# Issuing the sums of feed-forward values in one go, with later VectorE weight parts queued behind them

## The chip, the cores and the metric

The kernel runs on one core of a Trainium2 chip. A core has TensorE (matrix products; PE in the profile, with PEld for its weight loads), VectorE (DVE), ScalarE (ACT), GpSimd (POOL) and SyncE (SP, which here only issues transfers). The engines run side by side, each takes its own instructions in the order in which they stand in its stream, and they wait for each other through semaphores. The metric is the device time of one execution in microseconds (us); the median of three timed runs stands for a kernel. The profile is one further execution, recorded by the hardware, with its own time.

## The reference

One inference step of a hybrid encoder layer over 576 token rows (512 of a prompt, 64 of a sample):

```python
h   = x @ W_in                                   # queries, keys, values of two kinds of heads
mix = concat(ForgettingAttention(h_A), IndexedSparseAttention(h_B))
x   = LN1(alpha * x + mix @ W_o)
hid = relu(x @ W_up) ** 2                        # 1024 -> 4096
x   = LN2(alpha * x + hid @ W_down)              # 4096 -> 1024
x   = x + sigmoid(x @ W_g + b_g) * (p @ W_ple)
```

All is float32. The change concerns the feed-forward part, the lines of `hid` and `W_down`.

## The kernel before, in words

Tokens lie along the free axis, features along the 128 partitions. To keep float32 precision each factor of a product is split into a high part (a rounded copy, made by ScalarE) and a low part (the rest, a subtraction, mostly made by VectorE), and a product is three matmuls for each of its slices of 128 features: high by high, high weight by low value, low weight by high value (`gemm`, line 298; the matmuls have line 305).

**The stage of seven products.** The feed-forward width is cut into 8 groups of 512 (`NG`, line 386). Groups 0 and 1 are done plainly (`up`, line 1421). From group 2 on a block of W_up, two by two sub-blocks over two by two halves of the tokens and features, is done with seven products instead of eight, in the manner of Strassen and Winograd; so is W_down for groups 0 to 5 (`G_DOWN`, line 387, groups 6 and 7 go plainly through `down_last`). `seven` (line 1496) runs a list of pairs; each pair is seven products in the order 11, t0, t1, 21, t3, t2, 22, each of 12 matmuls, pinned to that order on TensorE. An even and an odd group of up pairs (two pairs each, m = 0 and 1) are followed by four down pairs that consume them (line 1684 on): up pairs of groups 2 and 3, four down pairs, up pairs of 4 and 5, four down pairs, up pairs of 6 and 7. There are two places, then, at which the second up pair of an odd group (3 or 5) hands over to down pair 0.

**The values between.** After each product a hook of the pair may run (`P.posts`). In an up pair (`up_pair`, line 1552) the hook of t2 adds two partial results on VectorE (L1573), squares the positive part (L1575 on VectorE for odd groups) and calls `operands` (line 1357). For an odd group that makes, from this value v and the values F of the even group, the operands of the down pairs: the second sum s2 = -F[0] - v (L1389) and its two parts (ScalarE L1368, VectorE L1366), the first sum s1 = F[1] - v (L1391) and its parts, the parts of v itself ("22"), and later "12" and "s4" (L1396). The down pair's products read them in this way (`ROWS`, line 1494): 11 reads "11", t0 "s3", t1 "s2", 21 "12", t3 "s1", t2 "22", 22 "s4". In the profile the tile hC holds s1 and s2, hA s3 and 11, hB 12 and 22, hD s4.

**What sets the order.** The hooks don't issue most of this at once. `later(delay, fn)` puts it on a list; `drive` (line 86) advances a clock by one for every six matmuls, and at each tick takes up to three entries that are due. So the steps are spread over the ticks after the product. The order in which the code issues instructions is the program's order; then the scheduler of the framework makes each engine's stream. It may take an instruction with a later number first where it reckons it ready sooner; `tc.high_priority()` raises what is issued inside it, and `tc.issue_after(ins)` makes what is issued inside it, on the engine of `ins`, stand behind `ins` in the stream, without waiting for its end.

**The weights.** `Weights` (line 117) streams the weights in. Each pair takes four units of weights from three loads (`add_seven`, line 171): r1 (two halves added by an accumulating transfer of GpSimd, L210), r2 and r3. A unit has a high part (ScalarE, L149) and a low part (VectorE, L155). Unit u is made from r2 as loaded, u+1 from r1; then VectorE adds r1 into the first half of r2 (`t1`, L181) and that half into the second (`t2`, L184); u+2 is made from these sums, u+3 (half as wide) from r3. Products 11 and 21 read u, t0 and t3 u+1, t1 and t2 u+2, and 22 reads u+3 (`PLACE`, line 105). These are pieces in a queue of the code; `WT.step()`, called after every six matmuls of a product, issues at most one, when its load has had time to land and buffers are free (`open`, line 220; a low part waits two ticks behind its high part, and the next piece may pass it). The raw buffers and the five buffers of parts (`whl`) go round in rings; a raw buffer that comes free lets SyncE issue the next load (L208).

The products wait for the parts they read by themselves: where a part is late, TensorE stands still at that matmul.

Of the kernel before, what the change touches and what calls it, by code (L numbers as in the profile page):

```python
# [11 lines left out]
OP = mybir.AluOpType  # L12
# [24 lines left out]
def tile_hybrid_step(ctx: ExitStack, tc: tile.TileContext, I, O):  # L37
    nc = tc.nc
    PE, ACT, DVE, POOL, SP = nc.tensor, nc.scalar, nc.vector, nc.gpsimd, nc.sync
# [4 lines left out]
    def f(ap):  # L44
        return ap.bitcast(F32)
# [16 lines left out]
    def later(delay, fn):  # L62
        number[0] += 1
        evq.append((clock[0] + delay, number[0], fn))
# [42 lines left out]
    class Unit:  # L107


        def __init__(self, t, c, o=0):  # L110
            self.t, self.c, self.o = t, c, o
# [5 lines left out]
    class Weights:  # L117
# [3 lines left out]
        def __init__(self):  # L121
            self.cs, self.loads, self.pieces = [], [], deque()
            self.raw_ring, self.raw_own, self.hl_ring, self.hl_own = {1024: [], 512: []}, {}, [], {}
            self.hv, self.done, self.oldest, self.loaded = {}, set(), 0, 0
            self.was, self.lag = deque([(0, 0)]), 1

        def ring(self, pool, n_raw, n_hl, name, n_small=0):
            self.raw_ring[1024] += [(pool, f"{name}raw{x}") for x in range(n_raw)]
            self.raw_ring[512] += [(pool, f"{name}rs{x}") for x in range(n_small)]
            self.hl_ring += [(pool, f"{name}hl{x}") for x in range(n_hl)]  # L130
# [10 lines left out]
        def split(self, u, src, cuts, eng):  # L141
            lo_at = [0]

            def high(c):
                def fn():
                    if c is cuts[0]:
                        self.slot(u)
                        lo_at[0] = clock[0] + 2
                    ACT.copy(self.hv[u][:, 0, c], src["tile"][:, c])  # L149
                return fn  # L150

            def low(c):
                def fn():
                    t = self.hv[u]
                    eng.tensor_tensor(t[:, 1, c], src["tile"][:, c], f(t[:, 0, c]), OP.subtract)  # L155
                    if c is cuts[-1]:
                        self.done.add(u)
                return fn
            for c in cuts:
                self.piece(u, None, high(c), src)  # L160
            for c in cuts:
                self.piece(u, lo_at if len(cuts) == 1 else None, low(c), src)
# [8 lines left out]
        def add_seven(self, ap):  # L171

            u = len(self.cs)
            self.cs += [128] * 4
            r1 = self.source(ap[:, 0:1024], acc=ap[:, 1024:2048])
            r2 = self.source(ap[:, 2048:3072])
            r3 = self.source(ap[:, 1024:1536], room=512)
            lo, hi, all2 = slice(0, 512), slice(512, 1024), slice(0, 1024)

            def t1():  # L180
                DVE.tensor_tensor(r2["tile"][:, lo], r2["tile"][:, lo], r1["tile"][:, lo], OP.add)  # L181

            def t2():
                DVE.tensor_tensor(r2["tile"][:, hi], r2["tile"][:, hi], r2["tile"][:, lo], OP.add)  # L184
            self.split(u, r2, [all2], DVE)
            self.split(u + 1, r1, [all2], DVE)
            self.piece(u + 1, None, t1, r1, r2)
            self.piece(u + 2, None, t2, r2)
            self.split(u + 2, r2, [all2], DVE)
            self.split(u + 3, r3, [lo], DVE)  # L190
            return u
# [87 lines left out]
    WT = Weights()  # L279
# [812 lines left out]
    for x, tag in ((0, "k32"), (1, "t2")):  # L1092
        t = sb.tile([128, NT], F32, name="praw", tag=tag)
# [235 lines left out]
    HX, late = {}, []  # L1329

    def sets(g):

        if g >= G_DOWN:
            hid[g] = base.tile([128, 2, 4, NT], F32R, name="hidE", tag="AL") if g % 2 == 0 else \
                fb.tile([128, 2, 4, NT], F32R, name="hidO", tag="hidO")
            return
        names = ("s3", "11") if g % 2 == 0 else ("12", "22")
        t = base.tile([128, 2, 2, 4, HW], F32R, name="hA", tag="AL") if g % 2 == 0 else \
            fb.tile([128, 2, 2, 4, HW], F32R, name="hB", tag="hidO")
        for i, n in enumerate(names):  # L1340
            HX[n] = [t[:, i, x] for x in range(2)]
        if g % 2 == 0:
            HX["f"] = fs.tile([128, 2, 4, HW], F32, name="hF")
# [10 lines left out]

    owed = {}

    def operands(g, m, t, v):

        b = slice(2 * m, 2 * m + 2)
        tt = DVE.tensor_tensor  # L1360

        def split(n, v, d=0):
            owed[n] = owed.get(n, 0) + 1

            def low():
                tt(HX[n][1][:, b], v, f(HX[n][0][:, b]), OP.subtract)  # L1366
                owed[n] -= 1
            later(d, lambda: ACT.copy(HX[n][0][:, b], v))  # L1368
            later(d, low)

        if g >= G_DOWN:
            oh, ol = [hid[g][:, x, b, (A, B)[t]] for x in range(2)]
            later(0, lambda: ACT.copy(oh, v))
            later(0, lambda: DVE.tensor_tensor(ol, v, f(oh), OP.subtract))
            return
        F = [HX["f"][:, x, b] for x in range(2)]
        if g % 2 == 0:
            if t == 0:
                split("11", v)
            if t == (g == 0):  # L1380
                later(3, lambda: tt(F[0], F[0], F[1], OP.subtract))
                split("s3", F[0], 3)
            return
        if t == 1:
            if m == 0:
                later(0, more_sets)
                if g > 1:
                    later(0, last_set)
            later(0, lambda: DVE.scalar_tensor_tensor(F[0], F[0], -1.0, v, op0=OP.mult, op1=OP.subtract))  # L1389
            split("s2", F[0])  # L1390
            later(1, lambda: tt(F[1], F[1], v, OP.subtract))  # L1391
            split("s1", F[1], 1)
            split("22", v, 3)
            return
        split("12", v)
        later(2, lambda: tt(v, v, F[0], OP.add))  # L1396
        if g > 1:
            split("s4", v, 2)
        else:
            late.append(lambda: split("s4", v, 2))  # L1400

    def up_half(g, c, m, sl):
        t = (A, B).index(sl)
        r = lnp[0].tile([128, 2, 320], F32, name="relu", bufs=2)[:, :, :HW]
        out = HX["f"][:, t, c:c + 2]
        later(0, lambda: ACT.activation(r, m[:, :, :HW], AF.Relu))
        later(0, lambda: ACT.activation(out, r, AF.Square))
        operands(g, c // 2, t, out)
# [132 lines left out]
    def owe(P, fn):  # L1541
        def do():
            fn()
            P.left -= 1
        P.left += 1
        later(0, do)

    def settle(P):
        while P.left:
            pop_now()  # L1550

    def up_pair(g, m):

        P = Pair(U["P", g // 2, g % 2 * 2 + m], SX)
        b = slice(2 * m, 2 * m + 2)
        tt = DVE.tensor_tensor
        if m == 0:
            P.start = lambda: sets(g)

        def target(t):  # L1560
            return HX["f"][:, t, b] if g < G_DOWN and g % 2 == 0 else P.r[:, t]

        def t0():
            P.r = fs.tile([128, 2, 2, HW], F32, name="r", bufs=2)
            owe(P, lambda: ACT.copy(P.r[:, 1, 0], P.z))

        def t3():
            settle(P)
            with tc.high_priority():
                tt(P.r[:, 1, 1], P.e, P.r[:, 1, 0], OP.subtract)  # L1570

        def t2():
            tt(P.r[:, 1, 0], P.o, P.r[:, 1, 0], OP.add)  # L1573
            if g % 2:
                later(0, lambda: DVE.scalar_tensor_tensor(target(1), P.r[:, 1], 0.0, P.r[:, 1], op0=OP.max, op1=OP.mult))  # L1575
            else:
                later(0, lambda: ACT.activation(P.r[:, 1], P.r[:, 1], AF.Relu))
                later(0, lambda: ACT.activation(target(1), P.r[:, 1], AF.Square))
            operands(g, m, 1, target(1))

        def s21():
            later(0, lambda: ACT.activation(P.r[:, 0, 0], P.d, AF.Relu))

        def s22():
            later(0, lambda: ACT.activation(P.r[:, 0, 1], P.e, AF.Relu))
            later(0, lambda: ACT.activation(target(0), P.r[:, 0], AF.Square))
            operands(g, m, 0, target(0))
        P.posts = {"t0": t0, "21": s21, "t3": t3, "t2": t2, "22": s22}
        return P

# [153 lines left out]
    lo, hi = (0, 1, 2, 3), (4, 5, 6, 7)  # L1744
# [101 lines left out]
```

## Time and profile before

| | us |
|---|---|
| median of 3 runs | 765.42 (765.17 to 766.64) |
| the profiled execution, its own time | 766.22 |
| its span, first to last instruction | 764.5 |
| TensorE busy in it | 751.9 |
| VectorE busy | 571.8 |
| ScalarE busy | 472.8 |

The seven-product stage lies at about 382 to 653 us of the span. The two handovers to down pair 0 are at about 470 and 562 us.

How to read the rows: a line of the timeline has the start in us, the duration in us, the engine, the line of the kernel, the operation, output <- inputs with their shapes, the number of like instructions merged (x), and in brackets how long the engine had been idle before it, with what ended the wait. For merged instructions the duration reaches from the start of the first to the end of the last. Neighbouring instructions of one engine overlap a little, so the pitch from start to start is shorter than the duration. A row of the waits has the engine and line that waited, for whom, the total in us, how many times and the longest. A row of the windows has the stretch, its length, each engine's busy time with its count of instructions, the granted clock of TensorE (1.00 is full), and the share and rate of the transfers.

### The profile page before, as it was taken

How to read it: one execution, taken by the hardware profiler on the slowest of the kernel's cores; microseconds unless marked ns; L12 is line 12 of the kernel's file. 1: busy time of each engine (PE TensorE's matmuls, PEld its weight loads, DVE VectorE, ACT ScalarE, POOL GpSimd, SP SyncE). 2: the span in 40 equal slices, each digit the busy share in tenths (PEclk: the TensorE clock that was granted, in tenths of full speed). 3: DMA queues.
4: the chain of work that ended last, by engine and by line, in shares of the span. 5: the costliest groups of instructions: out<-in, count | busy, mean ns of one | idle time of the engine just before them, and what ended most of it. 6: DMA issues, size and time to landing. Idle time of an engine off the chain costs nothing.

```text
span 764.5 us, 14624 instructions
## 1 busy us (share of the span) xinstructions
PE 751.9 (98%) x5679; PEld 731.5 (96%) x5679; DVE 571.8 (75%) x1119; ACT 472.8 (62%) x931; POOL 109.8 (14%) x130
## 2 busy tenths in 40 slices
PE   9999999999999999999999999999999999999997
PEld 7999988999899999999999999999999999999997
DVE  6788888888777865779777579866898666657643
ACT  6589777897676635788654577435764466625451
POOL 7100324344241000100000000000000000011000
PEclk9999999999999999999999999999999999999999
DMA  8438344244222315352546666667667664730001
GB/s 288 167 70 150 128 134 122 93 139 176 78 85 86 114 58 173 111 177 80 123 110 176 148 159 172 148 164 180 155 149 178 152 154 152 288 111 30 28 29 69
DMA packets 38197, 101.35 MB, mean 133 GB/s; under 512 B 6000, under 2 KB 10224, under 8 KB 38000
## 3 DMA queue, kind: packets, MB, share of 16 engines
q1 hardware_dynamic: 34384, 87.61, 37.1%
q0 software_dynamic: 3456, 12.58, 10.1%
q8 instruction: 44, 0.72, 0.4%
q10 hardware_dynamic: 288, 0.22, 0.1%
q14 instruction: 25, 0.20, 0.1%
HBM read 85.26 MB, written 9.54 MB: 124 GB/s over the span
## 4 chain that ended last, share of the span: by engine, by line
PE 80%; DVE 12%; ACT 6%; issue 2%; DVEq 0%; ACTq 0%
PE g L305 39%; PE m L305 15%; PE n L305 13%; PE g L293 2%; PE T L56 2%; PE V L975 2%; DVE dbias L710 2%; DVE whl L155 1%; ACT xr L788 1%; DVE m L708 1%; ACT whl L149 1%; PE m L469 1%; PE m L483 1%; PE S L900 1%; PE S L898 1%
## 5 line engine op out<-in xcount | busy, mean ns | idle before, releaser
L149 ACT CAST whl<-wraw 128x1024 fp32r<-128x1024 f32 (+2 forms) x190 | 154.9, 828 | 83.9 <-PE g L305 50.0
L155 DVE TENSOR_TENSOR whl<-wraw,whl 128x1024 fp32r<-128x1024 f32 (+2 forms) x158 | 157.8, 1008 | 53.4 <-ACT whl L149 52.8
L305 PE MATMUL m<-AH,whl 128*128 128x288 f32 x736 | 176.7, 307 | 0.0
L305 PE MATMUL g<-BH,whl 128*128 128x288 f32 (+2 forms) x680 | 143.3, 298 | 0.0
L305 PEld LDWEIGHTS m<-AH,whl 128*128 128x128 f32 x736 | 126.4, 188 | 1.7 <-issue 1.0
L305 PEld LDWEIGHTS g<-BH,whl 128*128 128x128 f32 x680 | 111.1, 188 | 1.3
L305 PE MATMUL m<-AL,whl 128*128 128x288 f32 x368 | 108.8, 296 | 0.0
L305 PE MATMUL g<-BL,whl 128*128 128x288 f32 (+2 forms) x340 | 100.6, 296 | 0.3 <-DVE BL L1250 0.3
L305 PEld LDWEIGHTS m<-AL,whl 128*128 128x128 f32 x368 | 69.5, 189 | 0.6
L305 PEld LDWEIGHTS g<-BL,whl 128*128 128x128 f32 x340 | 64.0, 188 | 0.9 <-DVE BL L1250 0.7
L210 POOL DMA_DIRECT2D wraw<-in_w_dram x24 | 20.8, 866 | 287.1 <-DMA wraw<-in_w_dram 207.5
L913 ACT ACTIVATE sP<-sP,st 128x128 f32<-128x128 f32 (+4 forms) x72 | 39.4, 549 | 35.4 <-DVE st L908 35.3
L155 POOL TENSOR_TENSOR whl<-wraw,whl 128x512 fp32r<-128x512 f32 x32 | 42.2, 1334 | 90.1 <-ACT whl L149 74.9
L305 PE MATMUL m<-BH,whl 128*128 128x288 f32 x192 | 43.0, 302 | 0.0
L305 PE MATMUL g<-s,whl 128*128 128x288 f32 x288 | 42.1, 295 | 0.0
L305 PE MATMUL n<-BH,whl 128*128 128x288 f32 x192 | 42.0, 294 | 0.0
L305 PEld LDWEIGHTS g<-s,whl 128*128 128x128 f32 x288 | 39.5, 188 | 0.0
L56 PE MATMUL T<-ident,sP 128*128 128x128 f32 (+1 forms) x176 | 31.3, 273 | 1.5 <-DVE sP L922 0.6
L305 PEld LDWEIGHTS m<-BH,whl 128*128 128x128 f32 x192 | 32.0, 188 | 0.5 <-issue 0.3
L305 PEld LDWEIGHTS n<-BH,whl 128*128 128x128 f32 x192 | 32.0, 188 | 0.0
L1520 ACT ACTIVATE g<-n 128x288 f32<-128x288 f32 x24 | 9.5, 395 | 35.6 <-PE n L305 35.6
L305 PE MATMUL m<-BL,whl 128*128 128x288 f32 x96 | 28.3, 294 | 0.0
(331 smaller groups left out, 1664.3 us busy)
## 6 DMA issues: line engine op xcount, KB each, us to landing
wraw<-in_w_dram SPq DMA_DIRECT2D x48, 512.0 KB, 4.0
wraw<-in_w_dram POOLq DMA_DIRECT2D x24, 512.0 KB, 5.8
wraw<-in_w_qkv_dram SPq DMA_DIRECT2D x23, 512.0 KB, 3.7
wraw<-in_w_dram SPq DMA_DIRECT2D x24, 256.0 KB, 4.3
wraw<-in_w_up_dram SPq DMA_DIRECT2D x8, 512.0 KB, 3.9
wraw<-in_w_down_dram SPq DMA_DIRECT2D x8, 512.0 KB, 4.1
wraw<-in_w_gate_dram SPq DMA_DIRECT2D x8, 512.0 KB, 4.2
wraw<-in_w_o_dram SPq DMA_DIRECT2D x8, 384.0 KB, 3.0
```

The costliest lines, as they stand in the source:

```text
L56: PE.transpose(out, in_, ident[:n, :n])
L149: ACT.copy(self.hv[u][:, 0, c], src["tile"][:, c])
L155: eng.tensor_tensor(t[:, 1, c], src["tile"][:, c], f(t[:, 0, c]), OP.subtract)
L210: POOL.dma_start(t[:, :n], it["acc"], accum_op=OP.add)
L293: PE.matmul(ps, W(w, k, slice(0, 128)), a[:, k, sl], start=(len(terms) == 2 and n == 0), stop=False)
L305: mm = PE.matmul(ps, W(w, kw, wc), a[:, ka, cols], start=(first and i == 0), stop=(last and i == n - 1), skip_group_check=more)
L469: PE.matmul(mk[:, h, :HW], w0(part, k), a[:, k, h * HW:(h + 1) * HW], start=(k == 0 and i == 0), stop=(k == 7 and i == 2))
L483: PE.matmul(acc[b][:n[b], :304], a[:, k, b * 128:b * 128 + n[b]], ixw(part, k), start=(k == 0 and i == 0), stop=(k == 7 and i == 2))
L710: tc.keep_in_program_order(DVE.match_replace(out=s, in_to_replace=m, in_values=s, imm_value=GONE))
L913: ACT.activation(j["P"], j["P"], AF.Exp, bias=j["st"][:, 0:1], scale=-1.0, accum_out=j["st"][:, 2:3])
L975: PE.matmul(ps[r, x * 256 + c.start:x * 256 + c.stop], P["vt"][:, kb, r], t[:, hh, kb, c], start=(kb == 0), stop=(kb == n - 1))
L1520: ACT.mul(P.e, P.o, -1.0)
```

## The change

1. `operands` no longer issues the s2 sum, its high part, its low part and the s1 sum as four entries of the list. A function `sums` issues them one after the other: L1389's sum, the ScalarE copy, L1391's sum, and the low part of s2.
2. For the second pair (m = 1) of an odd group, `sums` runs at once in the hook of t2, with high priority, and so does the square L1575 ahead of it. For the first pair the square and `sums` stay entries of the list.
3. The add L1573 has high priority in odd groups.
4. The low part of s2 is kept as `WT.behind`. From then on every weight piece of VectorE (the low parts L155, and the sums L181 and L184 of the units) that the code issues is put behind that instruction in VectorE's stream.

```diff
@@ class Weights
+            self.behind = None
+
+        def queued(self, eng):
+            return tc.issue_after(self.behind) if self.behind and eng is DVE else ExitStack()
...
-                    eng.tensor_tensor(t[:, 1, c], src["tile"][:, c], f(t[:, 0, c]), OP.subtract)
+                    with self.queued(eng):
+                        eng.tensor_tensor(t[:, 1, c], src["tile"][:, c], f(t[:, 0, c]), OP.subtract)
...
             def t1():
-                DVE.tensor_tensor(r2["tile"][:, lo], r2["tile"][:, lo], r1["tile"][:, lo], OP.add)
+                with self.queued(DVE):
+                    DVE.tensor_tensor(r2["tile"][:, lo], r2["tile"][:, lo], r1["tile"][:, lo], OP.add)

             def t2():
-                DVE.tensor_tensor(r2["tile"][:, hi], r2["tile"][:, hi], r2["tile"][:, lo], OP.add)
+                with self.queued(DVE):
+                    DVE.tensor_tensor(r2["tile"][:, hi], r2["tile"][:, hi], r2["tile"][:, lo], OP.add)
@@ operands
-    def operands(g, m, t, v):
+    def operands(g, m, t, v, now=False):
...
-            later(0, lambda: DVE.scalar_tensor_tensor(F[0], F[0], -1.0, v, op0=OP.mult, op1=OP.subtract))
-            split("s2", F[0])
-            later(1, lambda: tt(F[1], F[1], v, OP.subtract))
+            def sums():
+                DVE.scalar_tensor_tensor(F[0], F[0], -1.0, v, op0=OP.mult, op1=OP.subtract)
+                oh, ol = [HX["s2"][x][:, b] for x in (0, 1)]
+                ACT.copy(oh, F[0])
+                tt(F[1], F[1], v, OP.subtract)
+                WT.behind = tt(ol, F[0], f(oh), OP.subtract).ins
+                owed["s2"] -= 1
+            owed["s2"] = owed.get("s2", 0) + 1
+            if now:
+                with tc.high_priority():
+                    sums()
+            else:
+                later(0, sums)
             split("s1", F[1], 1)
             split("22", v, 3)
@@ up_pair, the hook of t2
-            tt(P.r[:, 1, 0], P.o, P.r[:, 1, 0], OP.add)
+            with (tc.high_priority if g % 2 else ExitStack)():
+                tt(P.r[:, 1, 0], P.o, P.r[:, 1, 0], OP.add)
             if g % 2:
-                later(0, lambda: DVE.scalar_tensor_tensor(target(1), P.r[:, 1], 0.0, P.r[:, 1], op0=OP.max, op1=OP.mult))
+                def sq():
+                    DVE.scalar_tensor_tensor(target(1), P.r[:, 1], 0.0, P.r[:, 1], op0=OP.max, op1=OP.mult)
+                if m:
+                    with tc.high_priority():
+                        sq()
+                else:
+                    later(0, sq)
...
-            operands(g, m, 1, target(1))
+            operands(g, m, 1, target(1), g % 2 == 1 and m == 1)
```

## The prediction

> **What bounds the kernel now.** I read the page first: how long the span is, and which engine fills it.
>
> ```profile
> span 764.5 us, 14624 instructions
> ...
> PE 751.9 (98%) x5679; PEld 731.5 (96%) x5679; DVE 571.8 (75%) x1119; ACT 472.8 (62%) x931; POOL 109.8 (14%) x130
> ...
> wraw<-in_w_dram SPq DMA_DIRECT2D x48, 512.0 KB, 4.0
> wraw<-in_w_dram POOLq DMA_DIRECT2D x24, 512.0 KB, 5.8
> ```
>
> TensorE is busy nearly throughout, so only its waits can be won. Next came the waits of its weight loads between 381 and 653 us, the stage of seven-product pairs that the change touches.
>
> ```profile
> PEld n L305 <- DVE whl L155: 1.6, 2, 0.8
> PEld n L305 <- DVE hC L1366: 1.2, 2, 0.6
> PEld n L305 <- ACT hC L1368: 0.7, 2, 0.3
> ```
>
> Columns: total us, times, longest. Three kinds of wait, each twice: the stage has two places alike, where an odd group's second up pair hands over to the down pairs (near 470 and 562 us). The timeline of the first shows two stalls.
>
> ```profile
> 474.49 0.86 PEld L305 LDWEIGHTS n<-hC,whl 128*128 128x128 f32 x6
> 475.67 0.19 PEld L305 LDWEIGHTS n<-hC,whl 128*128 128x128 f32 x1 [0.32 <-ACT hC L1368]
> 476.46 0.70 PEld L305 LDWEIGHTS n<-hC,whl 128*128 128x128 f32 x5 [0.60 <-DVE hC L1366]
> 477.10 1.65 PEld L305 LDWEIGHTS g<-hB,whl 128*128 128x128 f32 x12
> 478.70 1.65 PEld L305 LDWEIGHTS g<-hC,whl 128*128 128x128 f32 x12
> ...
> 486.67 0.32 PEld L305 LDWEIGHTS n<-hC,whl 128*128 128x128 f32 x2
> 487.77 1.36 PEld L305 LDWEIGHTS n<-hC,whl 128*128 128x128 f32 x10 [0.77 <-DVE whl L155]
> 489.08 1.65 PEld L305 LDWEIGHTS g<-hB,whl 128*128 128x128 f32 x12
> ```
>
> An undisturbed product takes 1.60 us (477.10 to 478.70), so 0.133 a matmul. Product t1 of down pair 0 took 2.61 (474.49 to 477.10): 1.01 lost, waiting for s2's parts (tile hC). Product t1 of down pair 1 took 2.41 (486.67 to 489.08): 0.81 lost, waiting for its low weight part. Two places of 1.82 are 3.6 us, the most that any cure here can bring. The busy time by windows says what stands behind both stalls:
>
> ```profile
> 456.95:489.78 32.83, 31.81 (x235) 31.01 (x234) 32.61 (x48) 20.20 (x33) 2.58 (x3) 1.00 0.59 141
> ```
>
> VectorE (third figure) works 32.61 of 32.83 us; the granted clock (behind POOL's 2.58) is 1.00. VectorE has no slack over three pairs: idle time added to it here comes out at the second stall.
>
> **What the change does at the handover.** VectorE and ScalarE there:
>
> ```profile
> 467.89 0.69 DVE L184 TENSOR_TENSOR wraw<-wraw 128x512 f32<-128x512 f32 x1
> ...
> 469.56 1.22 DVE L155 TENSOR_TENSOR whl<-wraw,whl 128x1024 fp32r<-128x1024 f32 x1
> 470.69 0.45 DVE L1573 TENSOR_TENSOR r<-n,r 128x288 f32<-128x288 f32 x1
> 471.06 1.22 DVE L155 TENSOR_TENSOR whl<-wraw,whl 128x1024 fp32r<-128x1024 f32 x1
> ...
> 472.86 0.68 DVE L155 TENSOR_TENSOR whl<-wraw,whl 128x512 fp32r<-128x512 f32 x1
> ...
> 474.80 0.75 DVE L1366 TENSOR_TENSOR hB<-r,hB 128x576 fp32r<-128x576 f32 x1
> 475.65 1.43 DVE L1366 TENSOR_TENSOR hC<-hF,hC 128x576 fp32r<-128x576 f32 x2
> ```
>
> ```profile
> 470.04 0.62 ACT L149 CAST whl<-wraw 128x512 fp32r<-128x512 f32 x1 [0.32 <-PE n L305]
> ...
> 471.95 1.04 ACT L149 CAST whl<-wraw 128x1024 fp32r<-128x1024 f32 x1
> ...
> 474.95 1.24 ACT L1368 CAST hC<-hF 128x576 fp32r<-128x576 f32 x2
> ```
>
> Product t2 ends at 470.04 (ScalarE is released by it). The chain is L1573, L1575, L1389, a ScalarE copy, and the first L1366 of the pair at 475.65. Three weight parts (469.56, 471.06, 472.86) stood in its way. The changed code puts it ahead of them. Steps that wait for each other, against one that doesn't:
>
> ```profile
> 460.56 0.75 DVE L1575 SCALAR_TENSOR_TENSOR r<-r 128x576 f32<-128x576 f32 x1
> 461.35 0.76 DVE L1389 SCALAR_TENSOR_TENSOR hF<-hF,r 128x576 f32<-128x576 f32 x1
> 462.02 0.75 DVE L1391 TENSOR_TENSOR hF<-hF,r 128x576 f32<-128x576 f32 x1
> ...
> 653.86 0.45 DVE L1573 TENSOR_TENSOR r<-n,r 128x288 f32<-128x288 f32 x1
> 654.34 0.76 DVE L1575 SCALAR_TENSOR_TENSOR r<-r 128x576 f32<-128x576 f32 x1
> ```
>
> L1575 starts 0.48 after L1573 (0.11 more than the 0.37 from 470.69 to 471.06), L1389 starts 0.79 after L1575 (0.12 more than the 0.67 from L1389 to L1391). The copy: the two casts at 474.95 take 1.24, so 0.67 each, overlapping by 0.10; the first ends at 475.62, the low part starts 0.03 later. So: L1573 470.05, L1575 470.53, L1389 471.32 to 472.08, copy 472.11 to 472.78, low part 472.81 instead of 475.65; L1391 fills the wait for the copy. t1 needs it at 474.62: the first stall's 1.01 goes.
>
> [...]
>
> **What is queued behind it.** `queued` holds every weight part that the code issues after the chain. In `product`, t2's hook runs before product 22's first six matmuls, and `WT.step` issues one piece after every six. In the program of before the numbers of the instructions are: L1573 5911, the L155 of 469.56 5918, L184 5928, the L155s of 471.06 and of 472.86 5963 and 5973. So not only late parts are held: L184 and the L155 of 469.56 ran before t2 had ended, and now come after 472.81. The latter is the low part of unit u+1, which t0 of down pair 0 reads in its third matmul; L184 makes the sum from which both parts of u+2, for t1, are taken.
>
> ```profile
> 473.03 1.75 PE L305 MATMUL g<-hA,whl 128*128 128x288 f32 x12
> ```
>
> t0 wants u+1 at 473.03 + 2 x 0.133 = 473.30. Worked on with a pitch of 0.67 for L1366, 1.13 for L155 (469.56 to 470.69) and 0.63 for L184: u+1 473.48 to 474.70, so t0 waits 1.40. Then L184 474.61 to 475.30, cast of u+2 (1.05) to 476.38, its low part 476.41 to 477.63. t0's other ten matmuls end at 476.03; t1 waits 0.35 for the cast, and its third matmul (476.65) 0.98 for the low part. Together 2.73 in place of 1.01: 1.72 worse. With L184 put ahead of u+1, t0 waits to 475.33 (2.03) and t1 not at all: 1.02 worse. I take the first, the order of the code. A bound from below needs only the 1.40: no order makes it less than 0.39 worse, so a gain at this stall is excluded.
>
> **VectorE's debt.** When L1573 starts, at 470.05 instead of 470.69, 1.13 + 0.63 = 1.76 us of work is still owed that before was done: 1.76 - 0.64 = 1.12 behind. The steps add 0.11 + 0.12, and the wait for the copy 0.15, where before 0.10 went the same way (474.80 + 0.75 to 475.65): 1.40.
>
> ```profile
> 484.76 2.96 DVE L155 TENSOR_TENSOR whl<-wraw,whl 128x512 fp32r<-128x512 f32 x3
> ```
>
> The last of these three is what the second stall waits for; it ends at 487.72, with VectorE full up to it, so now at 489.12. TensorE comes there 1.72 late (its third matmul at 487.07 + 1.72 = 488.79) and waits 0.33 instead of 0.7. The place ends 1.40 later. With L184 first TensorE comes 1.02 late and waits longer; the same end. Two places: **2.8 us**. The profiled run took 766.22, so 769.0; it lies 0.80 above the median of 765.42, so on the median **768.2**.
>
> **Edits at nothing.** For a group's first pair the chain is issued two steps later (L1389 is 5796, L184 5795), so only u+2's and u+3's low parts are held.
>
> ```profile
> 458.46 1.22 DVE L155 TENSOR_TENSOR whl<-wraw,whl 128x1024 fp32r<-128x1024 f32 x1
> ```
>
> ```profile
> 458.75 0.62 ACT L149 CAST whl<-wraw 128x512 fp32r<-128x512 f32 x1 [0.53 <-PE n L305]
> ...
> 483.83 2.00 ACT L149 CAST whl<-wraw 128x1024 fp32r<-128x1024 f32 x2 [0.98 <-PE g L305]
> ...
> 491.01 1.05 ACT L149 CAST whl<-wraw 128x1024 fp32r<-128x1024 f32 x1 [1.21 <-PE g L305]
> ```
>
> ```profile
> 463.65 1.59 PE n L305 x12
> ```
>
> ```profile
> 475.04 0.85 POOL L210 DMA_DIRECT2D wraw<-in_w_dram  x1 [11.56 <-ACT hB L1368]
> ```
>
> t2 ends there at 458.75. By the same steps the chain's low part starts at 458.76 + 0.48 + 0.79 + 0.79 + 0.70 = 461.52, and u+2 is ready at 461.52 + 0.67 + 1.22 = 463.41; t1 asks at 463.65 + 0.27 = 463.92. Cover 0.51; if it is gone, each 0.1 of lateness costs 0.1. VectorE loses 0.30 (458.46 to 458.76), 0.11 and 0.15 there, which is hidden: all but the held parts is done at 470.69 - 1.76 + 0.56 = 469.49, and it waits for t2 at 470.05 anyway. Transfers: u+2's raw buffer comes free at 477.63 instead of 472.28; SyncE's load takes 4.0, so 481.6, and the next casts ran at 483.83: cover 2.2. u+1's comes free 3.92 later, so GpSimd's accumulating load goes out at 478.96 instead of 475.04 and lands 5.8 later, at 484.8, for the cast of 491.01: cover 6.2. A load later than that would hold TensorE up by as much.
>
> **Rivals.**
> 1. The second stall dissolves, because the three L155 at 484.76 come in another order (two of them, 1.73 us, aren't what t1 waits for). Then TensorE alone counts: 1.72 - 0.81 = 0.91, or 1.02 - 0.81 = 0.21 a place: 765.8 to 767.2. For: VectorE is later, so more is ready when it chooses. Against: L184 and its cast are as late. Chance 0.20.
> 2. Dearer: ScalarE takes the weight cast of 471.95 ahead of the chain's copy, as it does now. The copy starts at 471.95 + 1.04 - 0.10 = 472.89, 0.78 later, and so does all behind it: 2.18 a place, 769.8. Against: the chain has high priority. Chance 0.13.
> 3. Faster: L184 and u+1's low part stay ahead of the chain. It decides whether u+1 is done by 473.30. Then the chain starts at 470.69, its low part at 473.45, u+2 ends at 475.34 against a need at 474.89: the first stall shrinks to 0.45. With the debt (0.28) still called in at the second stall it is no gain; with that stall gone too, 0.56 + 0.81 a place, 762.7. The numbers 5918 and 5928 speak against. Chance 0.09.
> 4. The change does not do what it says: other ready VectorE work takes the place of the parts, and all comes out as before, 765.4. Chance 0.05.
> 5. TensorE's clock drops in the longer stall. The row above has 1.00 across 1.8 us of stalls. At half the clock, two products of 1.60 would add 3.2 a place: 774.6. [...] Chance 0.03.
>
> **The numbers.** The forecast has chance 0.50, its own range 767.0 to 769.4 (debt of 0.8 to 2.0 a place). 0.2% is 1.5 us, about what can be measured. Slower by more: nearly all of the forecast, rivals 2 and 5, a quarter of rival 1: 0.69. Within: rest of rival 1, rival 4, a little of the forecast and of rival 3: 0.24. Faster: 0.07. The range 765.8 to 770.2 leaves out rival 5, most of rival 3 and half of rival 4.
>
> **What would show it.** Right: t0 of down pair 0 waits about 1.4 on L155 (a wait of "g" on whl, which before has not), no wait on hC is left, L184 and the former 469.56 part stand behind the chain's L1366, VectorE shows an idle half microsecond just before L1573, and the last L155 before the second stall ends 1.4 later against the handover. Wrong: u+1's low part ahead of L1573, the debt absorbed before the second stall, or a time under 764.

## The result and the profile after

The changed kernel takes 774.78 us, median of 4 runs (773.26 to 775.68), beside 765.46 for the kernel before (765.17 to 766.64, 4 runs): ratio 1.0119 [1.0106, 1.0131]. The forecast was 768.2: the right side, and 6.6 us too little, outside its range. The profiled execution took 775.68, 9.46 more than that of before. Of all executions below two are left out, one of 804 us and one profiled one of 812, which ran at a lower mean clock (0.851 and 0.949).

Line numbers move with the change: matmuls L305 to L312, low weight parts L155 to L160, their casts L149 to L153, L184 to L191, L1573 to L1591, L1575 to L1594, L1389 to L1397, L1391 to L1400; s2's copy is now L1399 and its low part L1401; the other operand low parts are L1373.

The waits of TensorE's weight loads in the same stretch (381 to 653 us) of the kernel after:

```profile
PEld g L312 <- DVE whl L160: 4.1, 2, 2.1
PEld n L312 <- DVE whl L160: 4.1, 4, 1.2
PEld n L312 <- ACT whl L153: 1.7, 2, 1.0
PEld g L312 <- DVE Y L1635: 0.3, 1, 0.3
```

No wait on hC is left: the chain does what it was made for. In its place stand 9.9 us of waits for weight parts, against 3.5 in all before. TensorE's timeline at the first handover shows where:

```profile
463.67 0.42 PE L312 MATMUL n<-s,whl 128*128 128x288 f32 x2
465.11 1.60 PE L312 MATMUL n<-s,whl 128*128 128x288 f32 x10 [1.02 <-DVE whl L160]
...
474.50 0.43 PE L312 MATMUL g<-hA,whl 128*128 128x288 f32 x2
476.75 2.02 PE L312 MATMUL g<-hA,whl 128*128 128x288 f32 x10 [1.82 <-DVE whl L160]
479.11 0.85 PE L312 MATMUL n<-hC,whl 128*128 128x288 f32 x2 [0.34 <-ACT whl L153]
480.43 2.77 PE L312 MATMUL n<-hC,whl 128*128 128x288 f32 x10 [0.47 <-DVE whl L160]
483.00 2.45 PE L312 MATMUL g<-hB,whl 128*128 128x288 f32 x12
485.28 1.76 PE L312 MATMUL g<-hC,whl 128*128 128x288 f32 x12
...
493.25 1.77 PE L312 MATMUL n<-hC,whl 128*128 128x288 f32 x12
494.86 1.36 PE L312 MATMUL g<-hB,whl 128*128 128x288 f32 x9
```

The bracket leaves out the first part of a wait, in which the matmuls before it are still on record (two take 0.43 from 474.50, their pitch makes it 0.27), so I take starts: at 0.133 a matmul the third should start 0.27 after the first. t1 of the second up pair loses 465.11 - 463.67 - 0.27 = 1.17; t0 of down pair 0 1.98; its t1 479.11 - 476.75 - 1.33 = 1.03 for the cast and 480.43 - 479.11 - 0.27 = 1.05 for the low part. t1 of down pair 1 (493.25 to 494.86) loses nothing. The same at the second handover gives 0.91, 1.97, 1.02, 1.06 and 0. And something else: the ten matmuls from 480.43 took 2.57 and the next twelve 2.28, in place of 1.33 and 1.60. The windows give the reason (the figure behind POOL's is the granted clock):

```profile
476.00:478.00 2.00, 1.25 (x8) 1.25 (x9) 2.00 (x4) 1.36 (x2) 0.00 (x0) 0.92 0.30 33
478.00:480.00 2.00, 1.62 (x6) 0.92 (x4) 2.00 (x3) 1.05 (x1) 0.00 (x0) 0.50 0.66 229
480.00:482.00 2.00, 1.57 (x6) 1.57 (x7) 1.99 (x5) 0.67 (x1) 0.85 (x1) 0.50 0.85 168
482.00:484.00 2.00, 2.00 (x10) 2.00 (x10) 1.68 (x2) 0.40 (x1) 0.00 (x0) 0.50 0.94 211
484.00:486.00 2.00, 2.00 (x15) 2.00 (x15) 0.52 (x2) 0.52 (x1) 0.00 (x0) 0.87 0.87 170
```

The clock was halved for some 7 us. The 0.92 of the first row puts the start at about 477.7 (2.00 x 0.08 / 0.50 = 0.3 before 478): behind t0's wait, which ended at 476.75, and ahead of both waits of t1. Behind those it cost (2.57 - 1.33) + (2.28 - 1.60) = 1.92. VectorE at the same place:

```profile
471.51 0.46 DVE L1591 TENSOR_TENSOR r<-n,r 128x288 f32<-128x288 f32 x1 [1.05 <-PE n L312]
472.00 0.76 DVE L1594 SCALAR_TENSOR_TENSOR r<-r 128x576 f32<-128x576 f32 x1
472.79 0.76 DVE L1397 SCALAR_TENSOR_TENSOR hF<-hF,r 128x576 f32<-128x576 f32 x1
473.47 0.75 DVE L1400 TENSOR_TENSOR hF<-hF,r 128x576 f32<-128x576 f32 x1
474.14 0.76 DVE L1373 TENSOR_TENSOR hB<-r,hB 128x576 fp32r<-128x576 f32 x1
474.81 0.75 DVE L1401 TENSOR_TENSOR hC<-hF,hC 128x576 fp32r<-128x576 f32 x1
475.48 1.22 DVE L160 TENSOR_TENSOR whl<-wraw,whl 128x1024 fp32r<-128x1024 f32 x1
476.61 0.75 DVE L1373 TENSOR_TENSOR hC<-hF,hC 128x576 fp32r<-128x576 f32 x1
477.28 0.69 DVE L191 TENSOR_TENSOR wraw<-wraw 128x512 f32<-128x512 f32 x1
477.88 0.76 DVE L1373 TENSOR_TENSOR hB<-r,hB 128x576 fp32r<-128x576 f32 x1
478.55 1.82 DVE L160 TENSOR_TENSOR whl<-wraw,whl 128x512 fp32r<-128x512 f32 x2
```

VectorE idles before the chain (1.05, where I had put half a microsecond), and u+1's low part (475.48) and L191 stand behind L1401, as forecast. But three operand steps of 0.67 (L1373) are among them: one in the chain's wait for the copy, one ahead of L191, one ahead of u+2's low part, and u+3's low part passes u+2's (the first of the two at 478.55 is the half-wide one). By the order of the code they are the steps of 22, of s1 and of 12. The first two cost time. ScalarE's copy started at 473.68, took 0.67 and so ended at 474.35, but s2's low part started at 474.81, behind the step of 22; and the step of s1 put L191 off by 0.67. The third and u+3's low part cost 0.1 at most, since u+2's low part had to wait for its cast (ended 479.05) and started at 479.15 (478.55 + 1.82 - 1.22):

```profile
478.00 1.05 ACT L153 CAST whl<-wraw 128x1024 fp32r<-128x1024 f32 x1 [0.64 <-DVE wraw L191]
```

The first pair looks alike: an hB step in the chain and an hC step behind it, both ahead of u+2's low part.

```profile
459.20 0.46 DVE L1591 TENSOR_TENSOR r<-n,r 128x288 f32<-128x288 f32 x1 [0.47 <-PE n L312]
...
461.83 0.75 DVE L1373 TENSOR_TENSOR hB<-r,hB 128x576 fp32r<-128x576 f32 x1
462.50 0.75 DVE L1401 TENSOR_TENSOR hC<-hF,hC 128x576 fp32r<-128x576 f32 x1
463.16 0.75 DVE L1373 TENSOR_TENSOR hC<-hF,hC 128x576 fp32r<-128x576 f32 x1
463.83 1.82 DVE L160 TENSOR_TENSOR whl<-wraw,whl 128x1024 fp32r<-128x1024 f32 x2
```

### The profile page after: what moved, and what is told of

It reads as the page before. It is cut to its first block, busy times and chain, and to the rows that moved or that the text cites. A ratio compares the mean times of both kernels' runs of the same rounds, so it can differ in the third digit from the quotient of the medians.

```text
span 774.0 us, 14622 instructions
## 1 busy us (share of the span) xinstructions
PE 755.1 (98%) x5679; PEld 733.4 (95%) x5679; DVE 573.3 (74%) x1119; ACT 474.9 (61%) x931; POOL 109.8 (14%) x130
## 4 chain that ended last, share of the span: by engine, by line
PE 79%; DVE 13%; ACT 5%; issue 1%; DVEq 0%; ACTq 0%
PE g L312 39%; PE m L312 14%; PE n L312 14%; PE g L300 2%; DVE dbias L717 2%; PE T L56 2%; ACT xr L795 2%; DVE m L715 1%; PE V L982 1%; DVE whl L160 1%; PE m L476 1%; ACT whl L153 1%; PE m L490 1%; DVE sP L915 1%; DVE x L798 1%
## 5 line engine op out<-in xcount | busy, mean ns | idle before, releaser
L153 ACT CAST whl<-wraw 128x1024 fp32r<-128x1024 f32 (+2 forms) x190 | 155.3, 830 | 88.1 <-PE g L312 50.5
L160 DVE TENSOR_TENSOR whl<-wraw,whl 128x1024 fp32r<-128x1024 f32 (+2 forms) x158 | 157.9, 1009 | 49.4 <-ACT whl L153 48.8
L312 PE MATMUL m<-AH,whl 128*128 128x288 f32 x736 | 176.6, 307 | 0.0
L312 PE MATMUL g<-BH,whl 128*128 128x288 f32 (+2 forms) x680 | 143.3, 298 | 0.0
L312 PEld LDWEIGHTS m<-AH,whl 128*128 128x128 f32 x736 | 126.4, 188 | 1.7 <-issue 1.0
L312 PEld LDWEIGHTS g<-BH,whl 128*128 128x128 f32 x680 | 111.1, 188 | 1.3
L312 PE MATMUL m<-AL,whl 128*128 128x288 f32 x368 | 108.7, 295 | 0.0
L312 PE MATMUL g<-BL,whl 128*128 128x288 f32 (+2 forms) x340 | 100.6, 296 | 0.3 <-DVE BL L1257 0.3
L312 PEld LDWEIGHTS m<-AL,whl 128*128 128x128 f32 x368 | 69.5, 189 | 0.7
L312 PEld LDWEIGHTS g<-BL,whl 128*128 128x128 f32 x340 | 64.0, 188 | 0.9 <-DVE BL L1257 0.8
L160 POOL TENSOR_TENSOR whl<-wraw,whl 128x512 fp32r<-128x512 f32 x32 | 42.2, 1333 | 90.2 <-ACT whl L153 85.3
L312 PE MATMUL m<-BH,whl 128*128 128x288 f32 x192 | 42.9, 302 | 0.0
L312 PE MATMUL g<-s,whl 128*128 128x288 f32 x288 | 42.1, 295 | 0.0
L312 PE MATMUL n<-BH,whl 128*128 128x288 f32 x192 | 41.9, 294 | 0.0
L312 PEld LDWEIGHTS g<-s,whl 128*128 128x128 f32 x288 | 39.5, 188 | 0.0
L312 PEld LDWEIGHTS m<-BH,whl 128*128 128x128 f32 x192 | 32.0, 188 | 0.5 <-issue 0.3
L312 PEld LDWEIGHTS n<-BH,whl 128*128 128x128 f32 x192 | 31.9, 188 | 0.0
L312 PE MATMUL m<-BL,whl 128*128 128x288 f32 x96 | 28.3, 294 | 0.0
```

Of the source, the lines that this page charges most:

```text
L312: mm = PE.matmul(ps, W(w, kw, wc), a[:, ka, cols], start=(first and i == 0), stop=(last and i == n - 1), skip_group_check=more)
```

## The experiments

My theory after the result: the queue edges alone make the loss, through the low parts that t0 and t1 read, with operand steps between that I had not counted, and a clock drop on top. Rivals: the sums in one go cost something; VectorE's debt sets the end; the clock is only a shadow of the waits. The kernels were timed in three groups, each beside the kernel before: at 765.83 (the four of part 1), 765.45 (filled, as_assumed, in_order, hot_third) and 765.43 (filled_look, assumed_filled, in_order_only, u3_behind).

**1. Which part makes it.** Four kernels take the queue away in parts. no_queue keeps the sums and priorities and never sets the instruction to queue behind:

```diff
-                WT.behind = tt(ol, F[0], f(oh), OP.subtract).ins
+                tt(ol, F[0], f(oh), OP.subtract)
```

> The changed kernel without the queue: no weight part is put behind the chain, the sums and the priorities stay. Theory (the queue edges make the whole loss): VectorE's stream at the handover is then that of before but for one swap of two low parts, so 765.5 within 0.7, both old stalls back (about 1.0 at t1 of down pair 0, 0.8 at t1 of down pair 1), granted clock 1.00. Rival (issuing the sums in one go, or the priorities, cost by themselves): over 767.

765.66, ratio 1.0001 [0.9992, 1.001]. Its waits are those of before, line by line:

```profile
PEld n L312 <- DVE whl L160: 1.6, 2, 0.8
PEld n L312 <- DVE hC L1401: 1.2, 2, 0.6
PEld n L312 <- ACT hC L1399: 0.7, 2, 0.3
```

So the queue makes all of the loss, and the sums in one go by themselves do nothing that these runs can measure. queue_m0 and queue_m1 set it for the first or the second pair only:

```diff
+                low = tt(ol, F[0], f(oh), OP.subtract).ins
+                if not now:      # queue_m0; queue_m1: if now
+                    WT.behind = low
```

> Only the chain of an odd group's first pair sets the queue. Theory: t1 of the second up pair waits about 1.0, then the handover is that of before, about 1.0 and 0.8 of stalls, as TensorE and VectorE are late by about the same: 1.0 a place, 767.5. Granted clock 1.00. Rival (the first pair's queue is what hurts): over 771.

767.77, 1.0027 [1.0017, 1.0038]: 1.94 for the edit that I had costed at nothing.

> Only the chain of an odd group's second pair sets the queue. Theory: the wait at t1 of the second up pair (1.17 and 0.91 in the changed kernel) is gone, those at t0 (2.0) and t1 (2.1) of down pair 0 stay, the two old stalls (1.01 and 0.81) are gone: 2.3 a place, 4.6, so 770.1 with the clock at full, up to 772 if it drops again at one place. Rival (the first pair's queue is what hurts): under 768.

774.53, 1.0118 [1.0102, 1.0133], dearer than expected. Its profiled execution took 772.58 with a mean clock of 0.996 and one drop, at the second handover this time (0.83 from 562 to 582 us, 1.00 from 470 to 490). The three others took 774.20 to 775.27 at 0.991. So a drop can come at either place or, by the mean of 0.991, at both, and one more drop is worth about 2 us.

queue_lows leaves L181 and L184 (the sums of the weights) out of the queue:

```diff
-                with self.queued(DVE):
-                    DVE.tensor_tensor(r2["tile"][:, hi], ...)
+                DVE.tensor_tensor(r2["tile"][:, hi], ...)
```

> The sums L181 and L184 of the weight units are no longer queued, the low parts still are. Theory: u+2's high part is made early, so t1 of down pair 0 waits 0.2 instead of 2.1; t1 of the second up pair still about 1.0, t0 still 2.0; less the two old stalls of 1.82, or 1.0 if the second is still there: 1.4 to 2.2 a place, 768.3 to 769.9, the granted clock at 1.00 as the long stall is shorter. Rival (the low parts alone make the loss): over 772.

771.91, 1.0077 [1.0064, 1.009]. Without the drop it would nearly fit: one of its runs showed 0.999 and took 770.04, the four at 0.995 to 0.996 took 771.55 to 772.79. t0's wait is the same as in the full change (4.1 in two waits); t1's is smaller, since u+2's sum is there. The drop came all the same, at the first handover, with t0's wait (1.98, over at 476.21) as the only one in the stretch before it:

```profile
473.62:477.03 3.41, 1.59 (x12) 1.36 (x12) 3.41 (x6) 3.19 (x6) 0.00 (x0) 1.00 0.01 2
477.03:480.44 3.41, 3.41 (x16) 3.41 (x16) 3.41 (x6) 0.00 (x0) 0.07 (x1) 0.50 0.77 209
```

**2. The clock.** filled puts 28 matmuls into the waits at each place, whose results nothing reads:

```diff
+                for _ in range((fill[1] if i == 2 else fill[2] if i == n else 0) if fill else 0):
+                    tc.keep_in_program_order(PE.matmul(fill[0], W(0, 0, wc), aH[:, k0, cols], start=True, stop=True))
...
+            at = {"t0": (14, 7), "t1": (7, 0)}.get(n) if P in handed else None
```

> The changed kernel with 28 extra matmuls at each of the two handovers, put into the waits of down pair 0: 14 behind the second matmul of t0, 7 behind its last, 7 behind the second matmul of t1. They use the weights and values at hand and write to an unused half of a PSUM tile; nothing reads what they give. At 0.133 us each they take 1.87 of a wait of 1.97, and 0.93 + 0.93 of waits of 2.1. Theory (about 2 us of the 9.3 come from the granted clock, which falls to 0.50 for some 7 us behind the long wait, at one or two of the two places of a run): with TensorE kept busy the windows at both places show 1.00, the mean clock is 0.999 or 1.00, and the time falls by 2 to 772.0 to 773.2. Rival (the lower clock is only how a wait shows itself in the records, the waits alone make the time): 774.8 as before or up to 1 more, because the extra matmuls push t1's a little.

772.98, median of the four runs at a clock of 0.999 to 1.00 (772.76 to 773.72), ratio 1.0098 [1.0082, 1.0113]. The same kernel, profiled once more:

> The changed kernel with the 28 extra matmuls at each place (their results aren't read), for its profile: the first run's profiled execution had a lower clock throughout the whole span and says nothing of the places. Theory: the windows at both handovers show a clock of 1.00, and the products t1 and 21 of down pair 0 take what the waits leave, no longer 2.6 and 2.3 us for ten and twelve matmuls. Rival: the drop to 0.50 behind the handover is still there.

773.17. Its windows at the two handovers, and behind them those of the changed kernel:

```profile
476.00:486.00 10.00, 10.00 (x74) 9.75 (x74) 9.96 (x16) 3.85 (x6) 0.84 (x1) 1.00 0.67 172
568.00:578.00 10.00, 10.00 (x74) 9.63 (x73) 9.99 (x15) 5.82 (x10) 0.87 (x1) 1.00 0.49 129
```

```profile
476.00:486.00 10.00, 8.44 (x40) 7.75 (x41) 8.19 (x13) 4.00 (x6) 0.85 (x1) 0.66 0.72 162
568.00:578.00 10.00, 6.63 (x46) 5.92 (x45) 9.73 (x14) 6.47 (x11) 0.41 (x1) 1.00 0.24 76
```

With TensorE kept busy the drop is gone, and 28 matmuls more a place make the kernel 1.8 us faster (774.78 to 772.98; the single execution of 773.17 gives 1.6). The clock is a cost of its own; it explains 1.6 to 1.9 of the 9.3, no more.

**3. The order that the forecast took for granted.** as_assumed puts the low parts of s1 and of the 22 operand behind the chain:

```diff
-                tt(HX[n][1][:, b], v, f(HX[n][0][:, b]), OP.subtract)
+                with tc.issue_after(WT.behind) if WT.behind and n in ("s1", "22") else ExitStack():
+                    tt(HX[n][1][:, b], v, f(HX[n][0][:, b]), OP.subtract)
...
-            split("s1", F[1], 1)
-            split("22", v, 3)
+            split("s1", F[1], 3)
+            split("22", v, 5)
```

> The changed kernel with the order of the feed-forward low parts on VectorE that the prediction took for granted: the low part of the 22 operand and that of s1 go behind the chain (a queue edge, and two ticks later), so nothing stands in the chain's wait for the ScalarE copy; u+1's low part comes right behind s2's, L184 right behind that. Still ahead of u+2's low part stand two or three operand steps of 0.67 beside the cast of 1.05. Theory (what the prediction had wrong at the places is the operand low parts put between, 0.67 each): t0 of down pair 0 waits 1.3 in place of 1.97, t1 of the second up pair 0 to 0.3 in place of 0.9 to 1.17, t1 of down pair 0 still about 2: 1.5 a place less, so 3 us less, 771.8 if the clock falls as often as in the changed kernel, 769.8 if a wait of 1.3 leaves it at 1.00. The prediction's own sum with these steps known would be 768.2 + 2 x 0.9 = 770.0. Rival (VectorE's debt sets the end, whatever the order within it): waits move from t0 to t1 and to down pair 1, and the time stays within 1 of 774.8.

773.6, 1.0106 [1.0093, 1.012]: a miss in the time, a hit in the waits. At the first handover:

```profile
472.61 0.43 PE L312 MATMUL g<-hA,whl 128*128 128x288 f32 x2
474.43 1.59 PE L312 MATMUL g<-hA,whl 128*128 128x288 f32 x10 [1.39 <-DVE whl L160]
476.45 0.53 PE L312 MATMUL n<-hC,whl 128*128 128x288 f32 x2 [0.44 <-ACT whl L153]
478.17 1.60 PE L312 MATMUL n<-hC,whl 128*128 128x288 f32 x10 [1.19 <-DVE whl L160]
```

From the starts t0 waits 1.55 (forecast 1.40) and t1 0.69 + 1.45 (forecast 0.35 + 0.98; another weight cast on ScalarE ahead of u+2's, at 474.40, and VectorE's steps still ahead of u+2's low part make the rest). The second up pair's t1 waits for nothing. What kept the time up is new: TensorE, back sooner, meets a late transfer.

```profile
487.63 2.51 ACT L153 CAST whl<-wraw 128x512 fp32r<-128x512 f32 x3 [5.18 <-DMA wraw<-in_w_dram]
490.06 0.39 ACT L1533 COPY g<-n 128x288 f32<-128x288 f32 x1
```

ScalarE stands still 5.18 us for a weight transfer, then does three casts, and the copy of 490.06, for which t1 of down pair 1 waits, comes behind them: that product started at 490.50, 1.33 late. At the second handover the clock dropped instead. assumed_filled has the same matmuls in the waits as filled:

> The kernel with the order that the prediction assumed, with the same extra matmuls in down pair 0's waits (their results aren't read). Its profile before had waits of 1.55 (t0), 0.69 and 1.45 (t1) at each place, a stall of 1.33 at t1 of down pair 1 of the first place, behind a ScalarE copy queued after casts whose transfer came late, and at the second place a lower clock that cost about 1.6. Theory: with the clock at 1.00 the 1.6 go, 772.0; the stall of 1.33 stays. Rival (the clock costs nothing by itself): 773.6.

773.05, 1.0095 [1.0082, 1.0109], clock 0.998 to 1.00: in its profile the drop is gone, and the time hardly moved, because the copy (L1538 there) is now late at both places:

```profile
PEld n L312 <- ACT g L1538: 2.9, 2, 1.5
PEld n L312 <- DVE whl L160: 0.2, 1, 0.2
```

So the expectation of 772.0 missed: I had counted that stall at one place. Which of the transfers is late, and why, I did not trace further.

**4. A better order.** in_order has no queue behind the chain; later parts stand behind the low part of each u+2 instead (`third` holds those units):

```diff
+                        ins = eng.tensor_tensor(t[:, 1, c], src["tile"][:, c], f(t[:, 0, c]), OP.subtract).ins
+                    if u in self.third:
+                        self.behind = ins
...
-                WT.behind = tt(ol, F[0], f(oh), OP.subtract).ins
+                tt(ol, F[0], f(oh), OP.subtract)
```

> The sums in one go with their priorities, without the queue behind s2's low part; instead the low part of each unit u+2 is the instruction behind which later VectorE weight parts stand, so that u+3's and the next pair's u go behind u+2's. Theory (the second stall is an order of three low parts, two of which t1 does not read, 1.73 us): the second stall of 0.81 goes at both places, the first one (1.01) stays as it was: 765.4 - 1.6 = 763.8. Rival (VectorE's debt: with no slack over three pairs the stall moves to another part): 765.0 to 766.0, with a new wait on whl at 22 of down pair 0 or 11 of down pair 1.

763.95, ratio 0.9983 [0.9974, 0.9992]: a little faster than both kernels. The wait on whl is gone from the list, and only the first stall is left:

```profile
PEld n L315 <- DVE hC L1404: 1.2, 2, 0.6
PEld n L315 <- ACT hC L1402: 0.6, 2, 0.3
```

in_order_only makes that edit in the kernel before, without the sums in one go:

> The kernel before with one thing only: later VectorE weight parts stand behind the low part of each unit u+2; the sums and their priorities are as before. Theory (that order alone took the second stall away, and the sums in one go bring nothing): 763.9, the second stall 0.2 in place of 0.81, the first as before. Rival (the sums in one go are part of that gain): 764.7 or more.

764.27, 0.9985 [0.9976, 0.9994]; the gain belongs to u+2's place, and the two intervals nearly coincide, so none of it is shown for the sums in one go. hot_third keeps u+1's low part and L184 ahead, and gives u+2's low part priority behind the chain:

```diff
+                if now:
+                    WT.hot = True
+                    later(2, lambda: setattr(WT, "behind", low))
...
+                    with self.queued(eng), (tc.high_priority if hot else ExitStack)():
```

> The sums stay in one go with high priority, but the queue is taken away from the parts that t0 and t1 need: u+1's low part and L184 keep their places ahead of L1573, u+2's low part gets high priority right behind the chain, and later VectorE parts stand behind u+2's low part, in each pair, so that u+3's no longer passes it. Theory (the loss is made by u+1's and u+2's parts being held; a chain that goes past u+3's and the operand parts only is a gain): chain's low part at 473.45, u+2's low part to 475.34, so the first stall is 0.45 in place of 1.01; u+2 before u+3 at down pair 1 takes the second stall away (0.81). Together 1.4 a place at best, 762.7; 764.0 if half of the second stall comes back as VectorE's debt. Clock 1.00. Rival (VectorE is full over three pairs, so any gain at the first stall is called in at the second): within 0.5 of 765.4. Rival (any chain in one go is slower): over 766.5.

766.09, 1.0011 [1.0003, 1.002]. The first stall grew, from 1.01 to 1.56: the copy of the chain (L1403 there) came behind a weight cast, a square and the copy of a product's result, and u+2's low part, on which t1 now waits, stands behind the chain.

```profile
471.15 1.04 ACT L153 CAST whl<-wraw 128x1024 fp32r<-128x1024 f32 x1
472.09 0.69 ACT L1617 ACTIVATE r<-r 128x576 f32<-128x576 f32 x1
472.68 0.40 ACT L1539 COPY g<-n 128x288 f32<-128x288 f32 x1
473.00 0.67 ACT L1403 CAST hC<-hF 128x576 fp32r<-128x576 f32 x1
```

u3_behind is in_order with the low parts of u+3 and of the next u behind s2's:

```diff
+                    with self.queued(eng), (tc.issue_after(self.chain) if self.chain and u in self.fourth else ExitStack()):
```

> The kernel with later parts behind u+2's low part, and besides that the low parts of u+3 and of the next pair's u behind the low part of s2, while u+1's and u+2's are free to go ahead: in the stream u+2's low part now stands in the chain's wait for the ScalarE copy, and u+3's 0.61 no longer in front of it. Theory (only parts that t0 and t1 do not read should be queued behind the chain): s2's low part 0.5 earlier, the first stall about 0.5 in place of 1.0 at both places, 763.95 - 1.0 = 763.0. Rival (ScalarE's weight casts stand ahead of the chain's copy, as they do where the first stall grew to 1.4): no gain, 764 to 765.

766.06, 1.0009 [1.0, 1.0018]. Its waits are 2.9 us for whl (four times), 0.7 for hB and 0.5 for ScalarE: the first stall moved, in part to product 21, and the second came back. VectorE works 19.18 of 20.00 us there (470 to 490); here, moving its parts about only moved the stall.

## Why the prediction was wrong, step by step

From the first up pair to product 21 of down pair 1 the profiles of before and after differ by 5.47 at the first and 3.37 at the second handover, and by 0.6 outside them. Forecast: 1.40 each.

- **The kernel's limits and the chain.** Right. The steps of the chain came as worked out (0.48, 0.79 and 0.67): L1594 0.49 behind L1591; L1397, which waits for L1594, 0.79 behind that; L1400, which doesn't wait for L1397, 0.68 further.
- **What is queued behind it.** Right in kind: u+1's low part and L184 held, t0 waiting on whl, hC's wait gone. no_queue and queue_m1 show it. Wrong in size. The failed sentence is "u+1 473.48 to 474.70": I put the held parts right behind s2's low part and saw no other VectorE work there. s2's low part started 3.30 behind L1591, not 2.76, with the 22 step in the copy's wait (0.4), and the s1 step held L191, and with it u+2's cast, by 0.67; the step of 12 and u+3 passed u+2 at little cost. t0 lost 1.97 instead of 1.40, t1 2.08 instead of 1.33. as_assumed takes the step out of the chain and gives 1.55. Without clock and first pair the two places lost 2.38 (5.47 - 1.92 - 1.17) and 2.46 (3.37 - 0.91), together 2.0 more than the 2.8 forecast.
- **Edits at nothing.** The failed step is "Cover 0.51". The same two operand steps, those of 22 and s1, stood ahead of u+2's low part, and the stall was 0.91 and 1.17: 2.1 for two. (L1591 started 0.27 later than ScalarE's cast that I read as t2's end, at the first place only; no row says why.) queue_m0 costs 1.94.
- **VectorE's debt.** Wrong as a cause. It was to end at t1 of down pair 1; that wait is 0 in the profile after, so TensorE's own lateness set the end, as rival 1 had it for that stall. in_order shows that the 0.81 was a matter of order: with u+2 ahead of u+3 most of it goes. So the sum of 1.40 was worked out for an end point that was no longer the limit.
- **Transfers.** In the changed kernel no wait of ScalarE's weight casts there ends with a transfer, so the covers of 2.2 and 6.2 were not used up; TensorE came later by more than forecast. In as_assumed, and by its waits in assumed_filled, a late transfer became the next limit.
- **The clock.** A rival with chance 0.03, priced at 3.2 a place, came true in all four runs (by their means of 0.994 to 0.996), in the profiled one at one of two places, at 1.9. The chance was my estimate; all that a run had shown for it was the clock of 1.00 across stalls of 1.01 and 0.81 in the profile of before. The forecast's waits were 1.40 at t0 and 0.35 + 0.98 at t1; t0's alone, 1.98, came before the drop. That the rival's 774.6 lies next to the measured 774.78 is luck: with the clock held the kernel still takes 772.98.

Together 2.8 + 2.0 + 2.1 + 1.9 + 0.6 is 9.4, against 9.46 between the profiled executions. The parts are cut from that difference, so the sum proves nothing by itself, and the 0.6 outside the handovers wasn't traced.

## What to carry to other kernels

An edge that puts work behind an instruction moves everything that the program issues later past it, also what used to run early, and the scheduler fills the holes with whatever else is ready: list the whole stream of the engine between the edge and the first reader, not only the instructions that the edit names. Before pulling a late chain forward, ask which of the parts it passes has the earliest reader; here the parts of t0 and t1 came due before the chain's own result. The gain lay in the smaller edit, keeping u+2's part ahead of those that are read later (764.27 by itself, 763.95 with the sums in one go).

## What the runs showed of the hardware

TensorE's granted clock fell to 0.50 behind a single wait of 1.98 us: in the profile after from about 477.7 on, 0.9 behind the end of t0's wait and ahead of t1's two, and in queue_lows 0.8 behind the end of the same wait, where t1 hardly waits; in queue_m1 it was 1.1 behind, at 570.0, again ahead of t1's waits. In as_assumed it fell at 573.7, behind waits of 1.55, 0.69 and 1.45. A single wait of 1.56 (hot_third, mean clock 0.999) and waits of about 1 (queue_m0, 0.998 to 1.00) were not followed by it. In the 3.41 us before each drop TensorE was busy 1.59 (after, queue_lows, queue_m1) or 1.79 (as_assumed); the drops lasted 3.41 (queue_lows, as_assumed) or 6.83 (after, queue_m1). With nearly equal waits it came at the first handover in the profile after, at the second in that of queue_m1, and at both in other runs by their mean of 0.991.

What decides in which place it falls stays open. The busy time alone doesn't: at the other handover of the profile after, TensorE is busy 1.59 in the 3.41 us from 571.62 to 575.03, as much as before the drop, and the clock is 1.00 all the way from 564 to 582.

That matmuls whose results nothing reads can make a kernel faster, here by 1.8 us, was forecast before that run, and the run bears it out.
